# A two-level Strassen-Winograd matmul: one more product, the fifth of region (2,3), made of quarters and summed onto Y in PSUM

## The chip, the cores and the metric

The kernel runs on one core of one Trainium2 chip. The metric is the device time in microseconds. The engines are called PE (TensorE, the matmuls), PEld (its weight loads), DVE (VectorE), ACT (ScalarE), POOL (GpSimd) and SP (SyncE). SP, ACT and POOL issue the DMAs: queue q1 is SP's, q10 ACT's, q0 POOL's. All queues share 16 DMA engines.

## The reference

```python
a, b: 4096 x 4096 float32, drawn from a normal distribution; alpha = 0.01
x = np.matmul(a, b)
return np.where(x > 0, x, alpha * x)
```

## The kernel before

The output has four row groups of 1024 rows and four column blocks of 1024 columns. A **region** (g, j) is row group g against column block j. The first region is made while the inputs arrive; the other 15 follow in the order of the list `regions` (L505): (0,1), (0,2), (0,3), then (1,2), (1,0), (1,3), (1,1), then (2,2), (2,0), (2,3), (2,1), then (3,2), (3,0), (3,1), (3,3). A and B are rounded to float16, A when it is brought in and turned by DVE (L142), B by the DMA that loads it (L533, on POOL).

Each region is a 2 x 2 block product and uses Strassen's scheme in Winograd's form: seven products instead of eight. `PRODUCTS` (L653) lists them as (operand of A, half and column half of B): a11, a12, s2, s3, s1, a22, s4, where s1 to s4 are sums of blocks of A and the B operands are replaced in place by sums made on DVE (`b_sum`, L589). A product is 64 matmuls of 128 x 128 weights against 512 columns (`product`, L809), into four banks of PSUM. Four banks are called Y, the other four Z; the two sets change places from region to region. The third product (s2) and the fifth (s1) are added up in Y without being cleared in between; Y then goes to v (`add`, L975).

Some products are split once more by the same scheme into **seven quarter products** of 16 matmuls against 256 columns each (`quarter_product`, L752). In before these are: in the groups 1 to 3, the sixth (a22) and the seventh (s4) of every region but the last of groups 1 and 2; and the fourth (s3) of every region but the first of its group. For this,

- sums of quarters of the A operand are needed, four of them, `sx(1)` to `sx(4)`. `sums_of_a` (L701) makes those of a22 and s4 on DVE once a group and stores them in DRAM (L702, `kept_q`); they are loaded again, 512 KB each, in each region (`load_sums`, L744): a22's by SP into rooms that the fourth product's operands leave, s4's by ACT into rooms that the sixth's operands leave. Those of s3 stay in SBUF (`sums_of_s3`, L735), three of them in a quarter that is not needed itself (`x21`, of a22, s4 and s3); the fourth is kept in DRAM;
- sums of quarters of the B operand are needed in each region: t3 in place (`t3_of_b`, L681), then t2, t4 and t1 (`sums_of_b`, L687, L689, L691), each one DVE instruction;
- the quarter products must be added up: ACT copies a bank to SBUF (L836 to L844 in the fourth, L911 to L920 in the seventh), DVE adds others (L1133 for the fourth, L864 in the sixth, L917 to L923 in the seventh).

Work is put in order by hand (`manual_schedule`): each engine executes its instructions in the order of the program and waits for what each needs. SP and POOL, which issue DMAs, do likewise, so an issue that waits holds up those behind it. Around the change, the order in a region that is neither first nor last of its group is: products 1 to 3 wide; fourth in quarters; loads of a22's sums; sums of B for the sixth and `add_v` (L980); fifth wide; sixth and seventh in quarters. Meanwhile POOL fetches B's left half for the next region (L533) as the fourth and fifth products leave its buffers, and SP fetches its lower half from `kept_half` (L530) as the sixth and seventh do. SP also stores the results after the leaky ReLU on DVE (`leave`: L313, then L986), and loads the two halves of s2 for the next region (L771).

The last region of a group, here (2,1), is `turning`: it also brings in the next group's A. POOL fetches it in pieces (L133) into three buffers of the `a16` pool, shared with the quarter sums; DVE turns each (L142) and ACT squares it (L608), for a check of the value range. In (2,1) four squares of a block of B (L231) and their sums on DVE (L240 to L264) stand ahead of the first fetch. The fourth product is in quarters here too and reads x21's sums: its third quarter needs t4 (L689), which DVE makes after turning A's pieces.

```python
fetch_b(i + 1, [(0, 1)], (1, 0) if in_fourth else (0, 1) if turning and g else ks)
...
if in_quarters:
    t3_of_b(quarters_of_b(i, 1, 0))
    sums_of_b(quarters_of_b(i, 1, 0), tq)
    t3_of_b(quarters_of_b(i, 1, 1))
    add_v()
...
product(4, y, False)
...
    tq, sq = sixth_in_quarters(u2_pairs, [new_bank(zbank + mt) for mt in range(MT)], v_pairs, v, y, tq, sq)
```

Of the kernel before, what the change touches and what calls it, by code (L numbers as in the profile page):

```python
# [8 lines left out]
P = 128  # L9
DT = mybir.dt.float16  # L10
# [14 lines left out]
KC = 8  # L25
# [6 lines left out]
MT = 4  # L32
# [16 lines left out]
def kernel(  # L49
# [157 lines left out]
    def new_bank(i):  # L207
        return psum_pool.tile([P, NT], FP32, name="ps", tag=f"ps{i}")
# [103 lines left out]
    def leaky(t):  # L312
        nc.vector.scalar_tensor_tensor(t, t, alpha, t, op0=MULT, op1=MAX if alpha <= 1 else MIN)  # L313
# [347 lines left out]
    kept_q = {name: dram_pool.tile([4, P, QUARTER], DT, name=f"kept_q{name}") for name in ("a22", "s4")}  # L661
# [21 lines left out]
    def sums_of_b(y, to, some=(2, 4, 1)):  # L683
        tt = nc.vector.tensor_tensor
        f = lambda n: b_quarter(to[n])
        if 2 in some:
            tt(f(2), y[0, 1], y[0, 0], ADD)  # L687
        if 4 in some:
            tt(f(4), y[1, 0], f(2), SUB)  # L689
        if 1 in some:  # L690
            tt(f(1), y[1, 1], f(2), SUB)  # L691

    def sums_of_a(g, name, room):

        x = {key: q.rearrange("p c m e -> p c (m e)") for key, q in quarters_of_a(g, name).items()}
        made = {}

        def make(n, x0, x1, op):
            made[n] = room(n)
# [12 lines left out]
    def by_chunk(t):  # L712
        return t.rearrange("p c m e -> p c (m e)") if len(t.shape) == 4 else t.rearrange("p (c m) -> p c m", m=2 * HALF)
# [32 lines left out]
    def quarter_product(xq, yq, to, first=False, by_row=False, banks=1):  # L746
        order = [(c, m) for c in range(KC) for m in range(2)]
        if by_row:
            order = [(c, m) for m in range(2) for c in range(KC)]
        for c, m in order:  # L750
            rows = slice(m * P, (m + 1) * P)
            nc.tensor.matmul(  # L752
                to[m], xq[:, c // 2, rows, c % 2], yq[:, c, :],
                start=first and c == 0 and m < banks, stop=c == KC - 1, skip_group_check=True,
            )

    def into(bank):
        return [bank[:, m * HALF:(m + 1) * HALF] for m in range(2)]
# [24 lines left out]
    for i, (g, j) in enumerate(regions):  # L783
# [67 lines left out]
        def sixth_in_quarters(pairs, banks, v_pairs, v, y, tq, sq):  # L851
# [34 lines left out]
            following(1, sq[4])  # L886
            next_t[4] = tq[2]
            sums_of_b(y7, next_t, (4,))
            more(0, 1, other)
            quarter_product(sx(3), b[0, 1], into(one))  # L890
            following(3)
            more(1, 0, one)
            more(1, 1, one)
            quarter_product(x[1, 1], t(4), into(third), True)
            more(1, 0, third)
            next_t[1] = tq[4]
            sums_of_b(y7, next_t, (1,))
            return next_t, next_s

        def seventh_in_quarters(y, one, other, tq, sq):  # L900
# [81 lines left out]
        def leave(pairs, h, nt):  # L982
            for r, t in enumerate(pairs):
                leaky(t.rearrange("p m n -> p (m n)"))
                for m in range(2):
                    nc.sync.dma_start(place(g, h, 2 * r + m, j, nt), t[:, m, :])  # L986
# [39 lines left out]
        first_of_group = i == 0 or regions[i - 1][0] != g  # L1026
        in_quarters = g > 0 and not turning
        in_fourth = in_quarters and not first_of_group
        second_of_group = in_fourth and regions[i - 2][0] != g
        early = [measure(i, *block) for block in EARLY.get((g, j), [])]  # L1030
        for m in early[:1]:
            m.begin()
        if first_of_group and g:
            keep_s2(g)

        product(0, y, True)
        if second_of_group:
# [80 lines left out]
            b_sum(B(0, 0, k), B(1, 1, k), B(0, 0, k), SUB)  # L1118
        if late_ones:
            late_ones[0].end()  # L1120
        if in_quarters and first_of_group:
            sq = {4: t[:, 3]}
            sums_of_a(g, "a22", lambda n: sq.setdefault(n, sq[4] if n == 4 else new_a16()))
            keep_x21(g, "a22")

        z = [new_bank(zbank + mt) for mt in range(MT)]
        if in_fourth or turning and g:
            v_pairs, v, parts = fourth_in_quarters(z, tq, {**s3_rooms(g), 4: a_quarter(sx4)})
            if turning:
                for n in range(3):  # L1130
                    turn_a_in(0, 1, n)
            for to, bank in parts:
                nc.vector.tensor_add(to, bank, to)  # L1133
            if turning:
                add_v()
        else:
            product(3, z, True)
            v_pairs, v = keep(z, side)
        if in_fourth:
# [22 lines left out]
        if in_quarters:  # L1162
# [3 lines left out]
            add_v()  # L1166
            if final:
                good = next(judged)

        product(4, y, False)  # L1170
        if turning:
            new_s(g + 1, "s1")
        if in_quarters:
            tq, sq = sixth_in_quarters(u2_pairs, [new_bank(zbank + mt) for mt in range(MT)], v_pairs, v, y, tq, sq)
        else:
            add(v, y)
            leave(v_pairs, 1, 1)
# [8 lines left out]
        fetch_b(i + 1, [(0, 0)], ks)  # L1186

        if not in_quarters:
            product(5, z, g > 0)
# [111 lines left out]
```

## Time and profile before

| | |
|---|---|
| time, median of 3 runs | 1533.41 us (1532.85 to 1534.18) |
| the profiled execution's own time | 1537.09 us |
| its span, first to last instruction | 1535.2 us |
| PE busy | 1523.4 us, 99% |
| DVE busy | 1158.9 us, 75% |
| ACT, POOL busy | 425.5 us, 258.3 us |
| DMA packets | 351.26 MB, mean 229 GB/s |
| granted clock of PE | 1.0 throughout |
| region (2,0) | 879.40 to 971.45 us |
| region (2,3) | 971.45 to 1063.38 us |
| region (2,1) begins | 1063.38 us |

The times in the profile count from the first instruction of that one execution. A timeline's row holds a start, a length, the engine, the line, and the operation with its output and inputs, tiles named by the program (`ps` is a PSUM bank, `a`, `b`, `s`, `q`, `c` are tiles in SBUF), a count, and in brackets the idle time just before with what ended it. "PE" ends are modelled, so rows overlap by about 0.17 us; from start to start they are exact. A stretch's row holds its bounds and length, each engine's busy time with its number of instructions, then PE's clock, the busy share of the 16 DMA engines (above 1 where packets of several queues are under way in one engine) and the GB/s.

### The profile page before, as it was taken

What the parts mean: (1) busy time and instruction counts of PE and PEld (TensorE: products, weight loads), DVE (VectorE), ACT (ScalarE), POOL (GpSimd) and SP (SyncE); (2) the same over time, 40 slices, a digit from 0 to 9 for tenths busy, and PEclk for the clock granted to TensorE, in tenths of its full rate; (3) what the DMA queues carried; (4) which work ended last, traced back from release to release, by engine and by line L of the source; (5) the groups of instructions that cost most, each with busy time, mean ns of one, the idle gap of its engine ahead of it and who ended that gap; (6) DMA issues with size and microseconds to landing.
All of it is one profiled execution on the core that took longest, in us unless ns stands there. A gap on an engine that the chain in (4) does not pass through costs nothing. (4 is left out here: it accounts for less than half of the span.)

```text
span 1535.2 us, 21782 instructions
## 1 busy us (share of the span) xinstructions
PE 1523.4 (99%) x8667; PEld 846.8 (55%) x8667; DVE 1158.9 (75%) x1207; ACT 425.5 (28%) x730; POOL 258.3 (17%) x426
## 2 busy tenths in 40 slices
PE   9999999999999999999999999999999999999998
PEld 4444444444446567574544747557554475746656
DVE  4368867766699686768769798676987978687677
ACT  2201344646310213103551130312464103041210
POOL 5641110243202011022220001010331100101000
PEclk9999999999999999999999999999999999999999
DMA  9999895998879999899798939669899892949824
GB/s 246 183 212 209 232 280 174 177 195 177 223 284 280 252 288 272 249 288 259 168 284 272 319 147 207 268 154 323 168 228 298 230 345 75 292 160 193 306 97 140
DMA packets 192002, 351.26 MB, mean 229 GB/s; under 512 B 18705, under 2 KB 131601, under 8 KB 178834
## 3 DMA queue, kind: packets, MB, share of 16 engines
q0 software_dynamic: 119808, 112.22, 46.4%
q1 hardware_dynamic: 65458, 211.98, 37.1%
q10 hardware_dynamic: 6624, 25.56, 4.4%
q8 instruction: 70, 1.15, 0.3%
q14 instruction: 42, 0.34, 0.1%
HBM read 344.98 MB, written 114.82 MB: 300 GB/s over the span
## 5 line engine op out<-in xcount | busy, mean ns | idle before, releaser
L809 PE MATMUL ps<-b,a 128*128 128x512 f16 x2624 | 570.6, 379 | 0.0
L809 PE MATMUL ps<-b,s 128*128 128x512 f16 x2240 | 489.2, 379 | 0.4 <-DVE b L589 0.4
L809 PEld LDWEIGHTS <-a 128*128 128x128 f16 x2624 | 256.8, 98 | 307.6
L809 PEld LDWEIGHTS <-s 128*128 128x128 f16 x2240 | 219.1, 98 | 263.1 <-issue 1.2
L589 DVE TENSOR_TENSOR b<-b 128x4096 f16<-128x4096 f16 x104 | 234.7, 2287 | 47.1 <-DMA b<-in_b_dram 37.7
L533 POOL DMA_DIRECT2D b<-in_b_dram x128 | 94.9, 746 | 861.0 <-PE ps L752 436.8
L822 ACT COPY c<-ps 128x512 f32<-128x512 f32 x164 | 84.8, 596 | 468.1 <-PE ps L809 424.5
L142 DVE STREAM_TRANSPOSE a<-a 128x512 uint32<-128x512 uint32 (+2 forms) x120 | 127.2, 1108 | 100.8 <-DMA a<-in_a_dram 100.7
L133 POOL DMA_DIRECT2D a<-in_a_dram x252 | 137.5, 553 | 266.1 <-ACT junk L608 88.2
L752 PEld LDWEIGHTS <-q 128*128 128x128 f16 x1424 | 139.3, 98 | 16.8 <-issue 0.7
L608 ACT ACTIVATE junk<-a 128x512 bf16<-128x512 f16 x192 | 121.1, 631 | 98.6 <-DMA a<-in_a_dram 93.2
L313 DVE SCALAR_TENSOR_TENSOR c<-c 128x1024 f32<-128x1024 f32 (+2 forms) x123 | 141.7, 1194 | 3.4 <-ACT c L822 3.2
L231 ACT ACTIVATE sq<-b 128x2048 bf16<-128x2048 f16 x64 | 118.4, 1910 | 38.7 <-DVE sq L240 30.9
L975 DVE TENSOR_TENSOR c<-ps,c 128x512 f32<-128x512 f32 x140 | 87.5, 682 | 55.0 <-PE ps L809 41.7
L752 PEld LDWEIGHTS <-a 128*128 128x128 f16 x1200 | 117.4, 98 | 19.0 <-issue 1.4
L283 PE MATMUL ps<-b,a 128*128 128x512 f16 x512 | 112.5, 379 | 1.6 <-DVE a L142 1.0
L752 PE MATMUL ps<-b,q 128*128 128x256 f16 x784 | 92.0, 273 | 0.6 <-DVE c L864 0.6
L752 PE MATMUL ps<-b,a 128*128 128x256 f16 x752 | 88.3, 273 | 0.0
L283 PEld LDWEIGHTS <-a 128*128 128x128 f16 x512 | 49.6, 98 | 62.4 <-issue 1.8
L911 ACT COPY c<-ps 128x512 f32<-128x512 f32 x9 | 5.3, 587 | 269.8 <-DMA out_dram<-c 118.9
L752 PEld LDWEIGHTS <-s 128*128 128x128 f16 x624 | 61.1, 98 | 7.1
L864 DVE TENSOR_TENSOR c<-ps,c 128x512 f32<-128x512 f32 x80 | 52.3, 687 | 14.3 <-PE ps L752 14.3
(104 smaller groups left out, 904.1 us busy)
## 6 DMA issues: line engine op xcount, KB each, us to landing
b<-in_b_dram POOLq DMA_DIRECT2D x136, 512.0 KB, 11.7
out_dram<-c SPq DMA_DIRECT2D x240, 256.0 KB, 6.4
a<-in_a_dram POOLq DMA_DIRECT2D x244, 128.0 KB, 5.7
b<-kept_half SPq DMA_DIRECT2D x28, 1024.0 KB, 11.1
b<-kept SPq DMA_DIRECT2D x20, 1024.0 KB, 9.2
q<-kept_qs ACTq DMA_DIRECT2D x40, 512.0 KB, 7.7
s<-kept_s SPq DMA_DIRECT2D x18, 1024.0 KB, 7.7
q<-kept_qa SPq DMA_DIRECT2D x28, 512.0 KB, 7.8
```

The lines of the kernel that those rows point to most:

```text
L133: nc.gpsimd.dma_start(a16[32 * q:32 * q + 32], src.rearrange("(g i) w -> i g w", i=32))
L142: nc.vector.transpose(part.rearrange("p c m e -> p c (m e)").bitcast(U32) .rearrange("p c (g i) -> p g c i", i=32), src[:, :, i * n:(i + 1 ...
L231: nc.scalar.activation(to, self.parts[n], SQUARE)
L283: nc.tensor.matmul(ps, a_cols(at[0, h, u], c, mt, (h, u) == (0, 0)), bt[0, u, nt][:, c, :], start=first, stop=last,)
L313: nc.vector.scalar_tensor_tensor(t, t, alpha, t, op0=MULT, op1=MAX if alpha <= 1 else MIN)
L533: nc.gpsimd.dma_start(t[:, c:c + 4, :], b_rows(j, u, c, 4, nt, g > 0))
L589: nc.vector.tensor_tensor(f(to), f(x0), f(x1), op)
L608: nc.scalar.activation(junk, piece[:, q, :], SQUARE, accum_out=to[:, 4 * n + q:4 * n + q + 1])
L752: nc.tensor.matmul(to[m], xq[:, c // 2, rows, c % 2], yq[:, c, :], start=first and c == 0 and m < banks, stop=c == KC - 1, skip_group_chec ...
L809: nc.tensor.matmul(banks[mt], a_cols(t, c, mt, t is first_a), B(half, nt, k)[:, c, :], start=first and (k, c) == todo[0], stop=(k, c) == t ...
L822: nc.scalar.copy(kept[mt], banks[mt])
L975: nc.vector.tensor_add(to, bank, to)
```

## The change

In the region (2,3) alone (`FIFTH`), the fifth product is made of quarters (`fifth_in_quarters`):

- In (2,0), DVE makes the four quarter sums of s1 and SP stores them (4 x 512 KB): three right after the `b_sum`s of the third product, the fourth after the sums of the fourth product. In SP's order the stores stand between s3's store and the loads of a22's sums. They lie in the room `t` that also holds a22's fourth sum and the sums of B for the sixth.
- In (2,2), SP also stores the first sum of s3 (512 KB), since its room, x21 of a22, serves in (2,3) as a place for ACT's copies; in (2,1) it is loaded again in four DMAs, ahead of the second half of s2.
- In (2,3), the sums of B's first quarter block are made on DVE ahead of the fourth product's adds, SP loads s1's four sums where it loaded a22's, and a22's follow as the fifth's quarters release their rooms. The fifth's quarters that belong to one block alone go straight onto Y; three results that belong to several blocks are made in two other banks, copied to SBUF by ACT four times, and added onto Y by DVE, eight adds of 256 columns and two of 512.
- The sums of B for the sixth are made between those adds and in the sixth itself, t3 for the seventh and the second sum later in the sixth; v's result leaves in two halves instead of at once, the second at the end of the sixth; the second and third bank of the sixth are exchanged. `add_v` moves ahead of the fifth.

PE's order is the same but for the fifth's 64 matmuls of 512 columns, which become 112 of 256. POOL's order is the same.

```diff
+    FIFTH = {(2, 3)}
...
+            if n == 1 and g in [of for of, _ in FIFTH]:
+                nc.sync.dma_start(by_chunk(kept_s31), sx[1])
...
+        def fifth_in_quarters(y, one, other, tq, sq, between):
+            b = quarters_of_b(i, 0, 0)
+            x = quarters_of_a(g, "s1")
+            t = lambda n: b_quarter(tq[n])
+            sx = lambda n: a_quarter(sq[n])
+            onto = lambda r, n: [y[2 * r + m][:, n * HALF:(n + 1) * HALF] for m in range(2)]
+            rooms = by_chunk(x21(g, "a22")).bitcast(FP32)
+            rooms = [rooms[:, :2], rooms[:, 2:]]
+            def copied(bank):
+                rooms.append(rooms.pop(0))
+                nc.scalar.copy(rooms[1], pair(bank))
+                return rooms[1]
+            def more(r, n, room):
+                for m, to in enumerate(onto(r, n)):
+                    nc.vector.tensor_add(to, to, room[:, m])
+            quarter_product(x[0, 0], b[0, 0], into(one), True)
+            room = copied(one)
+            quarter_product(sx(4), b[1, 1], onto(0, 1))
+            more(0, 0, room)
+            next(between)
+            quarter_product(x[1, 1], t(4), onto(1, 0))
+            quarter_product(sx(2), t(2), into(one))
+            room = copied(one)
+            quarter_product(x[0, 1], b[1, 0], onto(0, 0))
+            more(0, 1, room)
+            next(between)
+            quarter_product(sx(1), t(1), into(other), True)
+            room = copied(other)
+            more(0, 1, room)
+            more(1, 1, room)
+            quarter_product(sx(3), b[0, 1], into(one))
+            room = copied(one)
+            for m in range(2):
+                to = pair(y[2 + m])
+                nc.vector.tensor_add(to, to, room[:, m].unsqueeze(1).to_broadcast([P, 2, HALF]))
...
             quarter_product(x[0, 1], b[1, 0], into(fourth), True)
-            leave(v_pairs, 1, 1)
+            if between:
+                next(between)
+            else:
+                leave(v_pairs, 1, 1)
...
+            if between:
+                t3_of_b(y7)
             sums_of_b(y7, next_t, (2,))
             more(0, 0, fourth)
+            if between:
+                leave(v_pairs, 1, 1, (0,))
...
             sums_of_b(y7, next_t, (1,))
+            if between:
+                leave(v_pairs, 1, 1, (1,))
...
+        if i and regions[i - 1] in FIFTH:
+            for c in range(KC // 2):
+                nc.sync.dma_start(by_chunk(x21(g, "a22"))[:, c], by_chunk(kept_s31)[:, c])
...
+        if s1_here:
+            sums_of_a(g, "s1", lambda n: t[:, n - 1], (1, 2, 3), s1_sums)
+        if in_fifth:
+            t5 = {2: t[:, 0], 4: t[:, 1], 1: t[:, 2]}
+            t3_of_b(quarters_of_b(i, 0, 0))
+            sums_of_b(quarters_of_b(i, 0, 0), t5, (2, 4))
...
+        if s1_here:
+            sums_of_a(g, "s1", lambda n: t[:, 3], (4,), s1_sums)
+        if in_fifth:
+            s5 = {n: t[:, 3] if n == 3 else new_a16() for n in (4, 2, 1, 3)}
+            load_sums("s1", s5, (4, 2, 1, 3))
...
+        if in_fifth:
+            fifth_in_quarters(y, new_bank(zbank + 3), new_bank(zbank + 1), t5, s5, between)
+            sq = {n: t[:, 3] if n == 3 else new_a16() for n in (1, 2, 4, 3)}
+            load_sums("a22", sq, (1, 2, 4, 3))
...
+        else:
+            product(4, y, False)
```

More of the change, by code (lines that the diff above doesn't have):

```diff
@@ L660 @@
     kept_s2 = dram_pool.tile([2, P, KC * RM], DT, name="kept_s2")
-    kept_q = {name: dram_pool.tile([4, P, QUARTER], DT, name=f"kept_q{name}") for name in ("a22", "s4")}
+    kept_q = {name: dram_pool.tile([4, P, QUARTER], DT, name=f"kept_q{name}") for name in ("a22", "s4", "s1")}
+    FIFTH = {(2, 3)}
+    kept_s31 = dram_pool.tile([P, QUARTER], DT, name="kept_s31")
     kept_s3 = dram_pool.tile([P, QUARTER], DT, name="kept_s3")
@@ L691, in sums_of_b, with sums_of_a @@
             tt(f(1), y[1, 1], f(2), SUB)
-    def sums_of_a(g, name, room):
+    def sums_of_a(g, name, room, some=(1, 2, 3, 4), made=None):
         x = {key: q.rearrange("p c m e -> p c (m e)") for key, q in quarters_of_a(g, name).items()}
-        made = {}
+        made = {} if made is None else made
         def make(n, x0, x1, op):
+            if n not in some:
+                return
             made[n] = room(n)
@@ L849, in fourth_in_quarters, with sixth_in_quarters @@
                 (0, 0, fourth), (0, 1, other), (0, 1, third), (1, 0, one), (1, 1, one))]
-        def sixth_in_quarters(pairs, banks, v_pairs, v, y, tq, sq):
+        def fifth_in_quarters(y, one, other, tq, sq, between):
[33 more added lines that the diff above has]
+                nc.vector.tensor_add(to, to, room[:, m].unsqueeze(1).to_broadcast([P, 2, HALF]))
+        def sixth_in_quarters(pairs, banks, v_pairs, v, y, tq, sq, between=None):
             b = quarters_of_b(i, 1, 0)
@@ L882, in sixth_in_quarters @@
             more(0, 1, one)
+            if between:
+                t3_of_b(y7)
             sums_of_b(y7, next_t, (2,))
             more(0, 0, fourth)
+            if between:
+                leave(v_pairs, 1, 1, (0,))
             quarter_product(sx(4), b[1, 1], into(other))
-            following(1, sq[4])
+            following(1, None if between else sq[4])
             next_t[4] = tq[2]
-            sums_of_b(y7, next_t, (4,))
+            more_t4 = lambda: sums_of_b(y7, next_t, (4,))
+            if not between:
+                more_t4()
             more(0, 1, other)
             quarter_product(sx(3), b[0, 1], into(one))
-            following(3)
+            following(3, sq[3] if between else None)
             more(1, 0, one)
@@ L897, in sixth_in_quarters @@
             sums_of_b(y7, next_t, (1,))
+            if between:
+                leave(v_pairs, 1, 1, (1,))
             return next_t, next_s
@@ L980, in add_v, with leave @@
                 nc.vector.tensor_add(f(to), f(to), f(more))
-        def leave(pairs, h, nt):
+        def leave(pairs, h, nt, some=(0, 1)):
             for r, t in enumerate(pairs):
+                if r not in some:
+                    continue
                 leaky(t.rearrange("p m n -> p (m n)"))
@@ L1028 @@
         in_fourth = in_quarters and not first_of_group
+        in_fifth = (g, j) in FIFTH
+        s1_here = j == 0 and g in [of for of, _ in FIFTH]
         second_of_group = in_fourth and regions[i - 2][0] != g
@@ L1131 @@
                     turn_a_in(0, 1, n)
-            for to, bank in parts:
+            for n, (to, bank) in enumerate(parts):
+                if in_fifth and n == 2:
+                    sums_of_b(quarters_of_b(i, 0, 0), t5, (1,))
                 nc.vector.tensor_add(to, bank, to)
-            if turning:
+            if turning or in_fifth:
                 add_v()
@@ L1161, with for_the_sixth @@
             next(judged)
-        if in_quarters:
+        def for_the_sixth():
+            y6 = quarters_of_b(i, 1, 0)
+            t3_of_b(y6)
+            yield
+            sums_of_b(y6, tq, (2, 1))
+            yield
+            sums_of_b(y6, tq, (4,))
+            yield
+        between = None
+        z6 = range(MT)
+        if in_fifth:
+            tq = {2: t[:, 1], 1: t[:, 0], 4: t[:, 2]}
+            between = for_the_sixth()
+            z6 = (0, 2, 1, 3)
+        elif in_quarters:
             t3_of_b(quarters_of_b(i, 1, 0))
@@ L1166 @@
             add_v()
+        if final and not in_fifth:
+            good = next(judged)
+        if in_fifth:
+            fifth_in_quarters(y, new_bank(zbank + 3), new_bank(zbank + 1), t5, s5, between)
+            sq = {n: t[:, 3] if n == 3 else new_a16() for n in (1, 2, 4, 3)}
+            load_sums("a22", sq, (1, 2, 4, 3))
             if final:
                 good = next(judged)
-        product(4, y, False)
+        else:
+            product(4, y, False)
         if turning:
@@ L1173 @@
         if in_quarters:
-            tq, sq = sixth_in_quarters(u2_pairs, [new_bank(zbank + mt) for mt in range(MT)], v_pairs, v, y, tq, sq)
+            banks = [new_bank(zbank + n) for n in z6]
+            tq, sq = sixth_in_quarters(u2_pairs, banks, v_pairs, v, y, tq, sq, between)
         else:
@@ L1185 @@
             fifth.end()
-        fetch_b(i + 1, [(0, 0)], ks)
+        fetch_b(i + 1, [(0, 0)], (1, 0) if in_fifth else ks)
         if not in_quarters:
```

4 lines of the change are left out of this document (3 added, 1 removed).

## The prediction

> **What bounds the kernel now.** I read the page's head first, then PE's timeline around the change, then VectorE's (DVE) timeline behind PE's next gap, last the DMA rows by stretch. Regions are named (row group, column block); those that matter are (2,0), (2,3), which is changed, and (2,1), which also brings in A for the next group.
>
> The page, then PE's timeline from the fourth product of (2,3) to that of (2,1):
>
> ```profile
> span 1535.2 us, 21782 instructions
> ...
> PE 1523.4 (99%) x8667; PEld 846.8 (55%) x8667; DVE 1158.9 (75%) x1207; ACT 425.5 (28%) x730; POOL 258.3 (17%) x426
> ```
>
> ```profile
> 1025.11 13.98 PE L809 MATMUL ps<-b,s 128*128 128x512 f16 x64
> 1038.93 1.91 PE L752 MATMUL ps<-b,a 128*128 128x256 f16 x16
> 1040.67 1.91 PE L752 MATMUL ps<-q,q 128*128 128x256 f16 x16
> ...
> 1104.82 3.66 PE L752 MATMUL ps<-b,a 128*128 128x256 f16 x32
> 1109.70 1.91 PE L752 MATMUL ps<-q,a 128*128 128x256 f16 x16 [1.23 <-DVE q L689]
> ```
>
> PE sets the time: it is busy for 99% of the span, and a microsecond saved on it counts as long as no gap takes it back. The fifth product of (2,3) is the first row, 64 wide matmuls from 1025.11 to 1038.93. The first gap behind it stands at 1109.70, in (2,1): PE waits for the sum t4 (L689). What is saved ahead of that gap is kept only if t4 comes earlier too. VectorE ahead of it:
>
> ```profile
> 1090.38 2.11 DVE L142 STREAM_TRANSPOSE a<-a 128x512 uint32<-128x512 uint32 x2 [2.49 <-DMA a<-in_a_dram]
> 1092.82 2.10 DVE L142 STREAM_TRANSPOSE a<-a 128x512 uint32<-128x512 uint32 x2 [0.33 <-DMA a<-in_a_dram]
> 1094.85 2.44 DVE L975 TENSOR_TENSOR c<-ps,c 128x512 f32<-128x512 f32 x4
> ...
> 1108.42 1.23 DVE L689 TENSOR_TENSOR q<-b,q 128x2048 f16<-128x2048 f16 x1
> ```
>
> It waits for two pieces of A (2.49 and 0.33 us) and then works without a pause until t4. So t4 is set by the landing of A's third piece at 1092.8, not by PE. What sets that landing is in the rows by stretch (the last two columns are the DMA engines' busy share and GB/s):
>
> ```profile
> 926.00:954.00 28.00, 28.00 (x197) 18.97 (x195) 22.14 (x23) 1.76 (x3) 5.92 (x8) 1.00 1.08 216
> 1018.00:1046.00 28.00, 28.00 (x196) 18.98 (x195) 20.36 (x22) 1.76 (x3) 5.91 (x8) 1.00 1.10 220
> 1046.00:1062.00 16.00, 16.00 (x149) 14.33 (x148) 9.46 (x12) 1.17 (x2) 0.00 (x0) 1.00 1.03 384
> 1062.00:1074.00 12.00, 12.00 (x65) 6.08 (x63) 9.60 (x12) 8.67 (x7) 0.00 (x0) 1.00 0.96 359
> 1074.00:1078.00 4.00, 4.00 (x20) 1.82 (x19) 3.81 (x8) 1.62 (x4) 2.54 (x5) 1.00 0.49 97
> 1078.00:1093.00 15.00, 15.00 (x72) 6.77 (x70) 12.01 (x10) 5.68 (x16) 6.12 (x12) 1.00 1.06 194
> ```
>
> From 1018 to 1093 the DMA engines are full but for some 2.5 us: 0.51 x 4 in 1074 to 1078 and 0.04 x 12 before. A's pieces are issued from 1074.46, just as the queue of SyncE (SP) has run dry.
>
> **The change part by part.** Times are the trace's; the region's old clock is kept until the new part sets another.
>
> PE. A quarter product takes 1.745 us (1038.93 to 1040.67 to 1042.42 in the timeline); seven, as in the sixth product, took 1038.93 to 1051.15, 12.22 us. The wide fifth took 13.82. Saved: **1.60 us**, all on the path.
>
> The fifth's feeding in (2,3). VectorE gains four sums of B (L681 to L691, 1.22 us each), eight adds of 256 columns onto Y in PSUM and two of 512. No row of before writes PSUM from VectorE. The nearest, L940, reads PSUM and has 256 columns: 0.42 us; L864 with twice the columns is 0.69. Bounds 0.3 and 0.69; I take 0.42, and 0.69 for the wide ones. Laid in the new order behind the sums that ended at 1020.83: t3, t2, t4 to 1024.5; the first add of the fourth frees bank "one" at 1025.2, where PE is due at 1025.1 (**+0.1**); t1, the other adds and add_v to 1030.9; the first adds onto Y to 1031.8, where the fifth quarter (due at 1032.1) waits for them. The next two wait for that quarter's end, 1034.0; the last end at 1040.5. The sixth product's fourth quarter then needs L864's read of its bank at about 1042.3, due at 1042.7. Cover 0.3 to 0.4 us each time; at 0.69 an add both are lost by about 1 us, at 0.3 nothing is gained. ACT's four copies (0.59, L840) lie under PE's quarters. Cost: 0.
>
> The loads of s1's quarters take the places of a22's, behind the same releases of PE (1018.3, 1020.1, 1021.8, 1023.6; those in before landed by 1021.7, 1030.7 and 1032.8 for the first, third and fourth), and are needed at 1026.9, 1030.4, 1033.8 and 1035.6: hidden by 2 to 5 us. The a22 quarters follow as the fifth frees their rooms, at 1028.7, 1032.2, 1035.6 and 1037.4, needed at 1039.1, 1042.6, 1044.3 and 1046.1. With L744's landing of 8.3 to 9.2 us in these stretches that is +1.1 to -0.6 us of cover: 0, at worst 0.6.
>
> (2,0). Four sums of s1 (L701, 1.22 us each, 4.9 us) delay VectorE until about 946.9, and the add it then owes starts at 946.55 in before, since it sat idle for 3.68 us there: 0.3 us, off the path. SP matters more. The four stores stand ahead of a22's four loads, the fourth store waits for a sum at 938.6, and the fourth load also waits until that store has left its room. The loads move from 926.4-931.6 to 938.9 and later; needed at 948.7, 952.2, 954.0 and 955.7. With 2.1 MB of stores first, I put the landings at 945 to 953: cover of 1 to 4 us; a price of 0 to 2 if it is gone. I take 0.
>
> The split of v's store. Its first half leaves at about 1049.5, not from 43.28 on; ACT's copy in the seventh (L911) needs it landed by 1056.5, 7 us later (L986 took 6.8 to 9.2 there): 0 to 1. Its second half leaves at 1055.4, and SP's loads of kept_half for (2,1) queue behind it: issued at 1056.1, not at 1047.85; needed at 1075.6. Nothing on the path, but no DMA time is gained.
>
> (2,1): the DMA time. Between 1018 and the landing of A's third piece 2.10 MB of s1 and 0.52 MB of the reload of x21 are added: 2.62 MB at the 384 GB/s of the row 1046 to 1062 are 6.8 us. Idle time takes up 2.5. Mixed queues take up more. For the earlier region where A met a full SP queue, the DMA answer of 687 to 711 says:
>
> ```profile
> DMA packets 3399, 7.93 MB, mean 330 GB/s; under 512 B 380, under 2 KB 1847, under 8 KB 2872
> ## 3 DMA queue, kind: packets, MB, share of 16 engines
> q1 hardware_dynamic: 1754, 6.41, 71.6%
> q0 software_dynamic: 1642, 1.50, 37.2%
> ```
>
> 6.41 MB at 0.384 and 1.50 MB at 0.14 (the answer of 1076.5 to 1092.7, q0 nearly alone with A: 1.89 MB in 81.6% of 16.2 us) are 27.4 us of work in 24, 12% gained. Over the 20 us in which A now meets SP's queue, and on the 5 us of loads beside B's pieces, that is about 2.8 us. Left: 6.8 - 2.5 - 2.8 = **1.5 us** by which A's third piece, t4 and PE's restart (1109.70) come later than before, though PE gets there 1.5 us sooner. Bounds: 4.3 without the gain from mixing, -1.5 if the queues had more room than their busy share says.
>
> In the same rows q0 sent as many packets as q1 (1642 to 1754) but a quarter of the bytes. The Trainium skill, "DMA: Bandwidth & Descriptors", section "Queues, rings and completion order", says that each engine goes round its queues packet by packet; by that rule, the trace agrees, A's short packets don't get half of the bytes beside SP's long ones and must nearly sit out its queue. By equal bytes A would be through sooner and the gain would stand, 1532.0; by the rule alone, with nothing gained from mixing, the time would be 1537.7.
>
> Sum: the saving of 1.5 on PE ends in the wait at t4, which grows from 1.23 to about 4.2 us; behind it PE is as late as t4: **+1.5 us**. The profiled execution's own time was 1537.09 (span 1535.2 and 1.9 around it); it would be 1538.6. The median of the runs shown is 1533.41, 3.7 lower, so **1534.9** there.
>
> **The rivals.**
> 1. *The gain stands.* A lands with PE's earlier clock, as its issue hangs on PE through ACT's squares; VectorE has 2.8 us of waiting ahead of it in which 1074's idle time helps. -1.5 and up to +0.1 for small waits: 1532.0. For it: in before A's first piece took 2.8 us, an empty queue. Against: the busy shares above. Chance 0.30.
> 2. *Slower: DMA time adds one for one.* Place: t4 in (2,1), if mixing gains nothing (the packet rule above speaks for it); price 4.3 us, 1537.7, up to 1539 with 1 us more from (2,0)'s late quarters (the seventh's last quarter of s4 lands at 967.66 for 969.70). It decides from the point where A's third piece lands 3.1 us later, at 1095.9. Chance 0.22.
> 3. *The change does not do what it says:* VectorE's adds onto PSUM cost 0.69 or more and hold PE twice in (2,3), by some 1 us each. As DMA isn't delayed by it, the wait at t4 shrinks by as much: 1534 to 1536. Chance 0.05.
>
> **How the numbers follow.** Forecast 0.43, between 1533.5 and 1536.4. Without 2 in 10 at the ends (the upper part of rival 2, little below -1.6): 1531.8 to 1537.9. By 0.2%, 3.07 us, about what a measurement of this kernel can tell from no change: faster needs more than the 1.60 and the 1.23 of the gap together: 0.02. Slower is rival 2: 0.22. Within: 0.76.
>
> **What would show it.** PE: seven rows of 1.745 us in place of 13.98, no gap over 0.3 us in (2,0) and (2,3); a gap at t4 in (2,1) of 3 to 6 us. VectorE: a longer wait for A at L142's second and third pair there. DMA: 1074 to 1078 at a share near 1, a22's loads in (2,0) issued after 938. Wrong if the gap at t4 stays near 1.2 (rival 1), or if PE stands in a fifth or sixth product for a load (L744) or an add.

## The result, and the profile after

The changed kernel took 1538.01 us (median of 7 runs, 1534.99 to 1540.80) where the kernel before took 1533.97 beside it (7 runs): ratio **1.0022**, 95% interval 1.0012 to 1.0031, or +3.4 us (+1.8 to +4.8). Measured once more beside later experiments (after_again) it was 1.0016 (1.0007 to 1.0024), +2.4 us. So it is a little slower, by about the 0.2% that a measurement of this kernel can tell. On the base of 1533.41 the first ratio is 1536.8 and the second 1535.9: 1.9 and 1.0 over the forecast of 1534.9. Both lie inside the wide range (1531.8 to 1537.9), the first just outside the narrow one (1533.5 to 1536.4).

Line numbers of the changed kernel are 2 to 80 higher than before's: the quarter products are L759, t4 is L691, ACT's copies in the seventh L974 and L978, the adds onto Y L878 and L899.

The page's head of the profiled execution (its own time 1537.85; before's was 1537.09):

```profile
span 1535.5 us, 21923 instructions
...
PE 1523.1 (99%) x8715; PEld 851.7 (55%) x8715; DVE 1171.8 (76%) x1225; ACT 427.9 (28%) x734; POOL 258.2 (17%) x426
```

PE's timeline, with the fifth of (2,3) from its first to its last quarter and the three rows with a wait from (2,0) to (2,1):

```profile
950.91 1.91 PE L759 MATMUL ps<-q,q 128*128 128x256 f16 x16
953.47 3.67 PE L759 MATMUL ps<-b,q 128*128 128x256 f16 x32 [0.66 <-DMA q<-kept_qa]
...
1024.86 1.91 PE L759 MATMUL ps<-b,s 128*128 128x256 f16 x16
...
1035.33 1.91 PE L759 MATMUL ps<-b,q 128*128 128x256 f16 x16
...
1057.52 3.65 PE L759 MATMUL ps<-q,q 128*128 128x256 f16 x32 [1.06 <-ACT c L974]
...
1110.80 1.91 PE L759 MATMUL ps<-q,a 128*128 128x256 f16 x16 [2.94 <-DVE q L691]
```

The copy of ACT that the second of these waits for was itself waiting for v's store:

```profile
1056.88 0.58 ACT L974 COPY c<-ps 128x512 f32<-128x512 f32 x1 [18.97 <-DMA out_dram<-c]
```

The fifth is seven rows of 1.745 us, from 1024.86 to 1037.08: 12.22. But there are three waits where before has one (1.23). PE's busy share on the page, 99% in both, can't show waits of this size. What shows them is the step from one row's start to the next, less the 1.745 or 3.49 us that the row takes without a wait (this is 0.17 more than the idle time in a row's brackets, since the modelled ends overlap):

| where | before | after | difference |
|---|---|---|---|
| fifth of (2,3) | 13.82 | 12.22 | -1.60 |
| its first quarter, for bank "one" | 0 | 0.24 | +0.24 |
| (2,0), sixth: a22's fourth quarter | 0 | 0.82 | +0.82 |
| (2,3), seventh: ACT's copy, behind v's store | 0 | 1.22 | +1.22 |
| (2,1), fourth: t4 | 1.39 | 3.11 | +1.72 |
| sum | | | **+2.40** |

The spans differ by 0.3 only: in this execution the changed kernel came to (2,0) 1.3 us earlier, by shorter waits near 69 and 490 us that no edit touches, and what follows PE's last matmul was 0.8 us shorter.

VectorE's timeline ahead of t4:

```profile
1085.11 2.10 DVE L142 STREAM_TRANSPOSE a<-a 128x512 uint32<-128x512 uint32 x2
1091.54 2.11 DVE L142 STREAM_TRANSPOSE a<-a 128x512 uint32<-128x512 uint32 x2 [4.33 <-DMA a<-in_a_dram]
1093.91 2.10 DVE L142 STREAM_TRANSPOSE a<-a 128x512 uint32<-128x512 uint32 x2 [0.26 <-DMA a<-in_a_dram]
...
1109.52 1.22 DVE L691 TENSOR_TENSOR q<-b,q 128x2048 f16<-128x2048 f16 x1
```

The wait for A's second piece went from 2.49 to 4.33; the chain behind the third piece is as long as before. The rows by stretch, with the DMA engines' busy share next to last:

```profile
1058.00:1074.00 16.00, 16.00 (x99) 9.37 (x97) 10.32 (x12) 9.87 (x9) 0.17 (x1) 1.00 1.02 401
1074.00:1078.00 4.00, 4.00 (x20) 1.83 (x19) 3.87 (x7) 1.25 (x3) 3.00 (x6) 1.00 1.05 363
1078.00:1094.00 16.00, 16.00 (x76) 7.22 (x74) 11.24 (x10) 5.28 (x15) 5.48 (x11) 1.00 1.06 212
```

The idle half of 1074 to 1078 (0.49 in before) is gone.

### The profile page after: what moved, and what is told of

Same layout as the page of the kernel before. It is cut to its first block, busy times and chain, and to the rows that moved or that the text cites. A ratio compares the mean times of both kernels' runs of the same rounds, so it can differ in the third digit from the quotient of the medians.

```text
span 1535.5 us, 21923 instructions
## 1 busy us (share of the span) xinstructions
PE 1523.1 (99%) x8715; PEld 851.7 (55%) x8715; DVE 1171.8 (76%) x1225; ACT 427.9 (28%) x734; POOL 258.2 (17%) x426
## 5 line engine op out<-in xcount | busy, mean ns | idle before, releaser
L816 PE MATMUL ps<-b,s 128*128 128x512 f16 x2176 | 475.2, 379 | 0.5 <-DVE b L589 0.5
L759 PEld LDWEIGHTS <-q 128*128 128x128 f16 x1488 | 145.5, 98 | 19.0 <-issue 1.2
L759 PEld LDWEIGHTS <-a 128*128 128x128 f16 x1200 | 117.4, 98 | 20.5 <-issue 3.1
L1038 DVE TENSOR_TENSOR c<-ps,c 128x512 f32<-128x512 f32 x140 | 87.5, 681 | 45.0 <-PE ps L816 31.8
L759 PE MATMUL ps<-b,q 128*128 128x256 f16 x816 | 95.6, 273 | 0.7 <-DMA q<-kept_qa 0.7
L759 PE MATMUL ps<-b,a 128*128 128x256 f16 x752 | 88.3, 273 | 0.0
L974 ACT COPY c<-ps 128x512 f32<-128x512 f32 x9 | 5.3, 586 | 258.2 <-DMA q<-kept_qs 121.6
L759 PEld LDWEIGHTS <-s 128*128 128x128 f16 x672 | 65.8, 98 | 7.8 <-issue 0.2
L759 PE MATMUL ps<-q,q 128*128 128x256 f16 x528 | 62.9, 273 | 1.1 <-ACT c L974 1.1
## 6 DMA issues: line engine op xcount, KB each, us to landing
b<-kept SPq DMA_DIRECT2D x20, 1024.0 KB, 10.1
```

The source lines that it names most:

```text
L759: nc.tensor.matmul(to[m], xq[:, c // 2, rows, c % 2], yq[:, c, :], start=first and c == 0 and m < banks, stop=c == KC - 1, skip_group_chec ...
L816: nc.tensor.matmul(banks[mt], a_cols(t, c, mt, t is first_a), B(half, nt, k)[:, c, :], start=first and (k, c) == todo[0], stop=(k, c) == t ...
```

## The experiments

There are three waits, so there are three edits that meet one each (late_reload, early_store, other_room). Further runs leave out s1's loads or VectorE's adds, put the reload alone into the kernel before, repeat a kernel, or combine the edits. The table gives PE's waits in the one profile of each kernel (idle time as in the rows' brackets, us, over 0.09, from (2,0) to (2,1)), and the times. The medians of the kernel before beside them were 1533.72 to 1534.19.

| kernel | (2,0) a22 | (2,3) head, B | (2,3) v's store | (2,1) t4 | median | ratio to before, 95% |
|---|---|---|---|---|---|---|
| changed, first | 0.66 | - | 1.06 | 2.94 | 1538.01 | 1.0022 (1.0012-1.0031) |
| after_again | - | - | 1.07 | 0.54 | 1535.32 | 1.0016 (1.0007-1.0024) |
| one_load | 0.93 | - | - | 0.85 | 1535.92 | 1.0017 (1.0007-1.0027) |
| late_reload | - | - | 1.05 | - | 1534.65 | 1.0001 (0.9992-1.0009) |
| early_store | 0.92 | - | - | 2.90 | 1538.91 | 1.0034 (1.0025-1.0043) |
| early_again | - | 1.30 | - | 3.48 | 1538.42 | 1.0032 (1.0021-1.0042) |
| other_room | - | - | 1.04 | 2.63 | 1536.54 | 1.0012 (1.0003-1.0021) |
| no_adds | 0.90 | - | 1.07 | - | 1538.29 | 1.0030 (1.0019-1.0041) |
| reload_and_room | - | - | 1.06 | - | 1534.47 | 1.0008 (0.9999-1.0016) |
| three | - | - | - | - | 1532.78 | 0.9993 (0.9985-1.0002) |
| all_four | - | - | 0.10 | - | 1533.30 | 0.9997 (0.9988-1.0006) |
| before_reload | - | - | - | - | 1533.77 | 1.0003 (0.9994-1.0012) |
| before_a_behind_t4 | - | - | - | - | 1534.11 | 1.0002 (0.9993-1.0010) |

**one_load**, s1's loads left out:

```
-            load_sums("s1", s5, (4, 2, 1, 3))
+            held = {1: s5[4], 2: s5[2], 4: s5[1], 3: s5[3]}
+            load_sums("a22", held, (1, 2, 4, 3))
...
-            load_sums("a22", sq, (1, 2, 4, 3))
+            sq = held
```

> Leaves out s1's four loads in (2,3): a22's sums are loaded once, earlier, and stand in for s1's in the fifth product, so the fifth is computed from other data; 2.1 MB less in (2,3), all else as in the changed kernel. Theory (the changed kernel pays in waits for DMA: 0.66 in (2,0), 1.06 in (2,3)'s seventh, 2.94 at t4): A's third piece lands 1 to 2.5 us earlier, the wait at t4 falls from 2.94 to 0.5-2.0, the wait in (2,0) stays, the time falls by 1 to 2.5 us to about 1.000 of before. Rival (A's chain is tied to its own steps, t4's gap grew only because PE gets there sooner): the wait at t4 stays at 2.9 and the time within 0.5 us of the changed kernel.

The wait at t4 is 0.85, and v's store landed 4.8 us after its issue, not 7.3, so the wait before the seventh's third quarter went too, which I had not expected. The ratio, 1.0017, is not apart from the changed kernel's two, and 0.85 at t4 is no less than the 0.54 of the changed kernel's second profile (below). So this run doesn't show what s1's loads cost at t4.

**late_reload**, the reload alone moved:

```
-        if i and regions[i - 1] in FIFTH:
-            for c in range(KC // 2):
-                nc.sync.dma_start(by_chunk(x21(g, "a22"))[:, c], by_chunk(kept_s31)[:, c])
         product(0, y, True)
...
         leave(u1_pairs, 0, 0)
+        if i and regions[i - 1] in FIFTH:
+            for c in range(KC // 2):
+                nc.sync.dma_start(by_chunk(x21(g, "a22"))[:, c], by_chunk(kept_s31)[:, c])
```

> The reload of x21 (0.52 MB in four loads) moves from the head of (2,1) to behind the store of the first product there, so that it is no longer queued ahead of A's pieces. Theory (DMA time ahead of A): A's third piece lands 0.5 to 1.4 us earlier, the wait at t4 falls from 2.94 to 1.5-2.4, the time by 0.5 to 1.4 us; the two other waits stay. Rival (A is held by its own chain): the wait at t4 stays at 2.9. Either could be spoiled by a new wait in the fourth product for the reload, which should have landed by 1112.

VectorE's and then PE's timeline of late_reload:

```profile
1087.57 2.12 DVE L142 STREAM_TRANSPOSE a<-a 128x512 uint32<-128x512 uint32 x2 [1.17 <-DMA a<-in_a_dram]
1090.17 2.10 DVE L142 STREAM_TRANSPOSE a<-a 128x512 uint32<-128x512 uint32 x2 [0.49 <-DMA a<-in_a_dram]
```

```profile
1103.37 3.66 PE L759 MATMUL ps<-b,a 128*128 128x256 f16 x32
1107.05 1.91 PE L759 MATMUL ps<-q,a 128*128 128x256 f16 x16
```

The wait for the second piece fell from 4.33 to 1.17, and the row at 1107.05 has no listed wait (0.19 by the step). By the ratios the edit is worth 2.3 to 3.2 us against the two measurements of the changed kernel, more than the 0.5 to 1.4 expected; its interval is apart from the first and just overlaps the second. At 384 GB/s the 0.52 MB would take 1.4 us.

**early_store** and, later, **early_again**, v's first half stored sooner:

```
+            if between:
+                leave(v_pairs, 1, 1, (0,))
                 t3_of_b(y7)
             sums_of_b(y7, next_t, (2,))
             more(0, 0, fourth)
-            if between:
-                leave(v_pairs, 1, 1, (0,))
```

> Only VectorE's order in (2,3)'s sixth changes: the first half of v is finished and stored ahead of t3 and t2 of the seventh, 2.4 us sooner. Theory: its store lands about 1054.4, ahead of ACT's copy, and the wait of 1.06 before the seventh's third quarter is gone (under 0.2). Whether the time falls too depends on t4: if A's pieces are held by full DMA, the wait at t4 grows from 2.94 to about 4 and the time stays; if A moves with PE, the time falls by up to 1.2 us. Rival (the wait at 1057.52 comes from VectorE's added work, not from the store): the wait stays above 0.8.

> The changed kernel with the first half of v's store 2.4 us sooner, once more, for a second profile: the first one's time (1538.91) stood above the changed kernel's although a wait was gone from its profile. Theory (the wait at t4 differs from one execution to the next by over 2 us and hides it): this time 1533.5 to 1537, no wait at 1056, at t4 0.5 to 5. Rival (the earlier store of v costs in (2,1) while the reload stands ahead of A): again over 1538, with a wait at t4 of 3 to 6 in most profiles.

The wait before the seventh's third quarter is gone in both, so it was the store's. But the time did not fall; both ratios stand above the changed kernel's two. The second profile lists these waits of PE from 930 to 1125 (total, times, longest):

```profile
PE ps L759 <- DVE q L691: 3.5, 1, 3.5
PE ps L816 <- DMA b<-in_b_dram: 1.3, 1, 1.3
```

At t4 PE waits 2.90 and 3.48 us, and there is a wait for B that no other profile has (below). This does not account for all: both profiled executions were among the faster of their kernel (1536.49 and 1537.08). The rival of early_again holds as far as the time and t4 go, though the intervals overlap with the changed kernel's first.

The slower executions come with a lower granted clock of PE. Its mean over an execution was 0.998 or 0.997 in 13 of these two kernels' 24 executions, which took 1540.4 us in the mean, and 0.999 or 1.0 in the other 11, which took 1537.3. A mean that low was measured in 2 of 18 executions of the changed kernel, and in none of the 67 of the six kernels in which the reload doesn't meet the rest of the change (late_reload, reload_and_room, three, all_four and the two built on before). The profile under other_room shows such a fall of the clock. Why it is more frequent with the early store stays open.

**other_room**, the shared room for the quarter needed last:

```
-            sq = {n: t[:, 3] if n == 4 else new_a16() for n in (1, 2, 3, 4)}
-            load_sums("a22", sq, (1, 2, 3, 4))
+            which = (1, 2, 4, 3) if s1_here else (1, 2, 3, 4)
+            sq = {n: t[:, 3] if n == which[3] else new_a16() for n in which}
+            load_sums("a22", sq, which)
...
-            following(1, None if between else sq[4])
+            following(1, None if between or s1_here else sq[4])
...
-            following(3, sq[3] if between else None)
+            following(3, sq[3] if between or s1_here else None)
```

> In (2,0) the room t[:,3], which s1's fourth store has to leave first, goes to the third of a22's quarters, loaded last, in place of the fourth; it is needed one quarter product (1.75 us) later. Theory: the wait of 0.66 at 953.47 is gone (under 0.1), (2,3) as a whole starts 0.8 us earlier, and the time falls by 0 to 0.8 us, by how far A moves along; the waits in (2,3) and at t4 stay within 0.8 us of 1.06 and 2.94. Rival (all of SP's loads are late there, not the one behind the shared room): a wait of 0.5 or more stays in the same place or moves to the last of the quarters.

There is no wait in (2,0), here and in the three later kernels with this edit; with the room as in the change, 4 of 7 profiles have it. The time is lower than the changed kernel's first, as expected, but the intervals overlap.

This profile is the only one in which the clock fell inside the kernel, right behind the wait at t4:

```profile
1109.18 3.48 PE L759 MATMUL ps<-q,a 128*128 128x256 f16 x16 [2.63 <-DVE q L691]
1112.50 1.91 PE L759 MATMUL ps<-q,s 128*128 128x256 f16 x16
```

```profile
1109.00:1112.40 3.40, 3.21 (x16) 2.29 (x16) 3.40 (x4) 0.00 (x0) 0.00 (x0) 0.51 0.24 45
```

The granted clock (the 0.51, third from the end) was half for 3.4 us, and the quarter product in it took 3.32 us from start to start where it takes 1.745 elsewhere. That is 1.6 us behind a wait of 2.8 (by the step); 3.4 us at half clock lower the mean of the whole span by 0.0011. In the three other profiles with a wait of 2.9 to 3.5 there (changed, early_store, early_again) the clock stayed at 1.0. That the wait brings the fall is inferred from the place and from the count above; no run tests it alone.

**after_again**, the changed kernel without an edit:

> The changed kernel as it is, for a second profile and a tighter time beside the others on one chip. Theory: a wait at t4 of 2 to 4 us, one of 0.5 to 1.5 before the seventh's third quarter in (2,3), one of up to 1 in (2,0)'s sixth; 1536 to 1538.5, ratio 1.0015 to 1.003. Rival (the single profile was not typical): one of the three waits is missing or another of over 0.5 us stands somewhere from (2,0) on.

PE's row at t4 in this second profile of the changed kernel:

```profile
1106.80 1.91 PE L759 MATMUL ps<-q,a 128*128 128x256 f16 x16 [0.54 <-DVE q L691]
```

The wait is 0.54 in place of 2.94, and there is none in (2,0), in an execution of 1534.36 against 1537.85. These waits come and go with the landing of transfers; only the one behind v's store is in both. My expectation of 2 to 4 at t4 was a miss, and one profile is not enough to size such a wait.

**reload_and_room** (both edits) and **three** (the early store too):

> The late reload and the other room, with v's store as in the changed kernel. Theory: the wait of 1.05 before ACT's copy in (2,3)'s seventh stays (0.6 to 1.3), those in (2,0) and at t4 are gone (under 0.3); the time is 0 to 0.8 us under that with the reload alone moved (1534.65), 1533 to 1534.7, and 1.2 above the three edits together. Rival (the earlier store of v costs more than it saves): this is the fastest of the four, at or under the three together.

> The three edits that met one wait each, together: the reload behind the first product's store, the first half of v's store 2.4 us sooner, and the shared room for a22's third quarter. Theory (three waits for transfers, 0.82 + 1.22 + 1.72 us against before, ate the 1.60 saved on PE; without them PE has no wait over 0.3 us from (2,0) to (2,1), and t4's old wait of 1.23 is gone as well): 1530.5 to 1533 where before has 1533.9, ratio 0.998 to 0.9995. Rival (executions other than the profiled one have waits that no profile showed; the earlier store of v was 1 us over the changed kernel though its profile had a wait less): the time is at or above that with the reload alone moved, 1534 to 1536.

Three has no wait from (2,0) to (2,1), and its interval (0.9985 to 1.0002) lies apart from both of the changed kernel's: the three waits, with what hangs on them, are what the change paid. It is the fastest of all, 1.1 us under before, though its interval (-2.3 to +0.3) just holds no change. Beside reload_and_room the early store gains 1.7 us by the medians, near the 1.2 of its wait, but these two intervals overlap. So with nothing ahead of A the store's edit seems to pay.

**before_a_behind_t4**, in the kernel before (A's fourth piece is turned behind the sums):

```
-        if g:
-            bring_a(0, 0, [3])
+        if g and turning:
+            fetch_a(0, 0, 3)
...
             sums_of_b(quarters_of_b(i, 0, 1), tq, (2, 4, 1))
+            turn_a_in(0, 0, 3)
```

> The kernel before with one edit: in (2,1) and the like regions of the other groups VectorE turns A's fourth piece behind the sums t2, t4 and t1 in place of ahead of them, 2.1 us of its work out of t4's way. Theory (t4's wait of 1.23 is the end of one chain on VectorE, from A's third piece on): the wait is gone and the time falls by 1.0 to 1.4 us, ratio 0.9991 to 0.9994. Rival (turning later keeps a room of A's longer, its next pieces come later and hold something behind t4): the wait goes elsewhere, and the time stays within 0.3 us or grows.

The wait is gone, the time isn't lower. Two things in this profile fit that. A's third piece landed 2.1 us sooner than in before's one profile, without any edit ahead of it, so before itself probably has the wait of 1.23 in some executions only. And in (2,2) PE lost 1.1 us behind ACT's copies (L822): the 128 matmuls from 784.25 took 28.74 us to the next row, where before's took 27.63. That is the rival's "the wait goes elsewhere" in this execution; all_four, with the same edit, doesn't have it.

**all_four**, this edit with the three:

> The three edits together and A's fourth piece turned behind t4 (2.1 us of VectorE's work out of t4's way). Theory: with the three alone t4 was ready only 0.3 us before PE; with 2.1 us more of cover no execution waits there: 1531 to 1532.8, ratio 0.998 to 0.9993, with a narrower spread. Rival (the turn put off holds one of A's rooms and something behind t4 pays, as small waits of 0.1 did at 798 in the kernel before with that edit): 1533 to 1534.5.

No wait is over 0.1, but the ratio is 0.9997 (0.9988 to 1.0006): the fourth edit adds nothing to the three that can be seen.

**before_reload**, the reload (and the store of kept_s31) put into the kernel before:

> The kernel before with the reload of x21 alone added at the head of (2,1) (and the store that feeds it): 0.52 MB in 512 packets of 1 KB, and none of s1's 2.1 MB in (2,3). Theory now (the reload alone makes A's third piece late): it lands 1 to 2.4 us later after the region's head than in the two profiles without it (29.32 and 27.26), the wait at t4 is 1.5 to 3, the time 0.8 to 2.4 us over before. Rival (my forecast's: A is late by the whole of the 2.62 MB, of which the reload is a fifth): the wait at t4 stays at 0 to 1.5 and the time within 0.5 us of before.

PE's rows around t4 there:

```profile
1103.09 3.66 PE L756 MATMUL ps<-b,a 128*128 128x256 f16 x32
1106.75 1.91 PE L756 MATMUL ps<-q,a 128*128 128x256 f16 x16
```

There is no listed wait (0.17 by the step), and the time is that of before. The theory that I held by then, that the reload alone makes A late, falls. It needs something of the rest of the change as well.

**no_adds**, without ACT's copies and VectorE's adds in the fifth:

```
-                nc.scalar.copy(rooms[1], pair(bank))
...
-                for m, to in enumerate(onto(r, n)):
-                    nc.vector.tensor_add(to, to, room[:, m])
+                pass
```

(and the two wide adds behind the last quarter).

> The changed kernel without ACT's three copies and VectorE's ten adds onto Y in the fifth product of (2,3): the terms they would carry are missing from the output there. VectorE is some 4.5 us less busy ahead of the seventh. Theory: PE waits for none of the adds, so nothing changes in the fifth; but VectorE reaches v's first store earlier, so the wait of 1.06 before the seventh's third quarter is gone (under 0.3); the wait at t4 stays at 0.5 to 3; the time falls by 0.6 to 1.2 us. Rival (VectorE's added work is what the whole change costs): the wait at t4 goes as well and the time falls by 2 to 3.5 us, to before's or below.

(The code makes four copies, not three, and all four are left out.) VectorE then waits for PE in the sixth, and v's store still leaves 13.3 us ahead of (2,1)'s head, as in the changed kernel: the wait of 1.07 stays, against what I expected. Less work on VectorE gains nothing, so its adds are not the cost. The time, 1.0030, is not explained: there are only 7 runs, and the profile also has waits of 1.59 at 69.66 and 0.63 near 95, ahead of anything that was edited.

**What settles t4.** In all 14 profiles A's first piece is issued 11.07 or 11.08 us after (2,1)'s first matmul, so A moves with PE. PE is due at t4's quarter 44.93 us after that first matmul. Where A's fourth piece is turned ahead of t4, t4 ends 16.95 us after A's third piece has landed (its end in the VectorE rows less the landing), and PE starts 0.06 later. So PE waits for whatever of the landing lies beyond 27.9. In the trace's DMA records:

| in the kernel | third piece landed after (2,1)'s head | mean |
|---|---|---|
| neither (before, before_a_behind_t4) | 29.32, 27.26 | 28.3 |
| reload alone (before_reload) | 28.08 | |
| rest of the change, reload late (late_reload, reload_and_room, three, all_four) | 28.12, 27.93, 27.88, 28.12 | 28.0 |
| reload ahead, 2.1 MB of loads less (one_load) | 28.94 | |
| both (changed, after_again, other_room, early_store, early_again, no_adds) | 31.03, 28.63, 30.72, 30.99, 31.56, 27.94 | 30.1 |

Each alone adds nothing to be seen (the reload alone in one profile only); both add 1.9 us in the mean, and from 0 to 3.4 in one execution. That fits idle time of the DMA engines ahead of A (some 2.5 us by the forecast's rows) that takes in either part and not both; this is inferred, the runs show only the landings. Nor do they say which part of the rest it is: s1's 2.1 MB of loads, or SP's queue, where v's second store half holds up the loads of kept_half (first issue at 1055.81, before 1047.85).

## Why the prediction was nearly right

**PE's saving.** Right: the fifth took 12.22 us, 1.60 less.

**VectorE's adds onto Y.** Right: one of 256 columns lasts 0.42 us and one of 512 0.69, as I took; in a row they overlap, so that four take 1.42 and two 1.28. PE never waits for one. Bank "one" cost 0.24 for 0.1. Rival 3 is out.

**The loads in (2,3).** Right: there is no wait for s1's or a22's quarters there in any profile.

**(2,0).** "A price of 0 to 2 if it is gone. I take 0" failed: 0.82 in the first profile. The order was as said: loads behind stores, the fourth behind its room. But the fourth left only at 944.32, when s1's fourth store had landed, took 9.1 us and landed at 953.43. That is 954.8 in before's clock, behind the due time of 954.0 and behind the 945 to 953 that I had guessed. In the mean of the seven profiles with this room the listed wait is 0.5 us. That PE stands in the sixth for such a load was one of the marks I had set for being wrong.

**The split of v's store.** "0 to 1", of which I took 0, failed: 1.22, and the same in all six profiles that have both the store at this place and s1's loads. Its second transfer takes 7.3 us each time and was needed after 6.1. I had 6.8 to 9.2 for it in the same sentence, and 7 us of time: that gives 0 to 2.2, so the bound was too narrow, and I took its lowest end.

**(2,1).** The mechanism fits: idle time and mixing take up most of the 6.8 us, and in the first profile the wait for t4 grows. By the sum's own terms (at 384 GB/s, less 2.5 and 2.8) s1's 2.1 MB alone would cost 0.2 us and the reload alone nothing, and neither shows a cost alone. By rival 2, with nothing gained from mixing, s1's alone would cost 3.0. (The 2.8 is rounded low: 12% of the 25 us named is 3.0, and the sum 1.3.) The size was off: the wait grew by 1.72, not by 3.0, and in after_again it is smaller than before's (0.71 against 1.39 by the step). I let the whole of PE's lead of 1.5 be lost there. But A's issue is bound to PE (11.08 in all profiles), as rival 1 said, so a lead would have moved along; and there was none left, since the waits ahead had used it up. That my 1.5 for A is near the pair's growth (1.72) and the means' (1.9) is in part luck: I meant it from before's clock, in which A's third piece landed 2.4 us later (29.32 to 31.03 behind a head that came 0.7 later), between the forecast's 1.5 and rival 2's 3.1.

**Sum.** +1.5 forecast; +2.4 in the profiled pair: 0.82 + 1.22 + 0.14 too little, 1.28 too much. Errors that partly cancel brought the time near, which was luck. The measured ratios, 1.0022 and 1.0016, lie on either side of the edge of "within 0.2%", to which I gave 0.76.

**What the forecast left out.** It has no term for B's loads in (2,0). POOL loads B for (2,3) while s1's stores and a22's loads run. The DMA queues from 933 to 962 (packets, MB, share of the 16 engines) and the time from issue to landing (median, us, last), first of before and then of after:

```profile
q0 software_dynamic: 3804, 3.77, 79.4%
q1 hardware_dynamic: 845, 2.25, 21.2%
...
b<-in_b_dram POOLq DMA_DIRECT2D x6, 512.0 KB, 10.0
```

```profile
q0 software_dynamic: 2328, 2.32, 49.4%
q1 hardware_dynamic: 1574, 4.89, 47.0%
...
b<-in_b_dram POOLq DMA_DIRECT2D x6, 512.0 KB, 17.4
```

q0, which has B, got 2.32 MB through in place of 3.77. B's last block landed 10.3, 4.6 and 6.4 us ahead of (2,3)'s head in the three kernels built on before, and 5.6 to 10.1 us after it in the eleven built on the change: 14 us later. It is needed some 8.7 us after the head (978.0 in early_again, where it landed at 979.3: the wait of 1.30). The ten other profiles were in time by 1 to 3 us. How often timed executions are not, no profile tells; it may be part of what is open in the early_store runs. Nor does the forecast have a term for the clock, which in other_room's profile cost 1.6 us behind the wait at t4.

## What to carry to other kernels

Where DMA is full around a change, price a transfer by its place and by what else is new beside it: 0.52 MB just ahead of the transfer that someone waits for cost 2 to 3 us here beside the rest of the change, and nothing once moved 29 us later or put into the kernel before alone. Follow every queue that runs beside the moved traffic, also those whose loads are needed a region later. Where a transfer's measured times (6.8 to 9.2 us) lie about or above the time that is left for it (7), don't put the wait at nothing. Behind a long wait of PE, look at its clock too. And two or three profiles of one kernel tell more of such a wait than one.

## What the runs showed of the hardware

Where A's loads met the second load of s2, the two queues were served packet for packet, not byte for byte. s2's packets have 8 KB, A's 1 KB: from 20 to 22 us after (2,1)'s head the trace has 74 such packets of A beside 77 of s2 in before, and 74 beside 82 in after_again. In these 2 us A moves 0.08 MB, where it moves 0.28 alone (before, 1079 to 1081). It is the rule that the prediction named from the Trainium skill, "DMA: Bandwidth & Descriptors", section "Queues, rings and completion order"; the trace agrees.

Transfers of one program land at different times from execution to execution: A's third piece 31.03 and 28.63 us after the head in the changed kernel's two profiles. Over all six kernels with both parts it is 27.94 to 31.56, over the four with the reload late 27.88 to 28.12.

In one profile the granted clock of PE was half for 3.4 us behind a wait of 2.8 us, and 16 matmuls of 256 columns took 3.32 us in place of 1.745 (other_room). A VectorE add that reads and writes PSUM lasted as long as one that reads PSUM and writes SBUF: 0.42 us with 256 columns, 0.69 with 512.
